# A depthwise convolution as a two-way filter on VectorE, its last tile one step earlier, and output banks evacuated in pairs

## The chip, the cores and the metric

The kernel runs on one core of one Trainium2 chip. The metric is the device time of one execution in microseconds (us); lower is better. Times of the kernel before: 845.77 us, the median of three runs from 844.53 to 849.2. One more execution was profiled, and every row below is from it.

## The reference

One layer of a hybrid decoder, for 1024 positions of a prompt and 8 single new positions of other sequences (1032 rows), with a model width of 1024. All arrays are float32.

```
h = rmsnorm(x) * norm_g
z = h @ w_in                       # 1024 -> 6144: a_val, a_gl, a_gate, b_u, b_v, b_gate
a_in   = a_val * sigmoid(a_gl)
a_conv = causal depthwise conv of a_in, 31 taps per channel, + conv_b
a_out  = silu(layernorm(a_conv)) * silu(a_gate)
gated  = W_s @ layernorm(b_v) + b_s      # per head, inside chunks of 128 positions
b_out  = b_u * gated * silu(b_gate)
y = rmsnorm(x + concat(a_out, b_out) @ w_out) * final_g
```

For the new positions the convolution continues from 30 stored rows, and the chunk has length 1. Outputs are y, the new convolution states and the v rows of the last chunk.

## The kernel before, in words

Channels lie on the 128 partitions, positions along the free dimension. The input projection is computed by a Strassen-like scheme with seven products (`PRODS`) over 2 x 2 blocks. Each float32 factor is split into a rounded head and a remainder (ACT makes the head, VectorE the remainder), and each product is made of three matmuls. `units` lists 24 steps: P (value and gate of the convolution branch, 128 channels), v (256 channels of b_v), B (b_u and b_gate of a head), G (256 channels of a_gate). A step has seven slots, one per product, of 24 matmuls each; in the slots of one step the weights of the next are summed (`wsum`) and split (`wsplit`), and weights of the step after are loaded (`wload`). The first slot of the next step finishes the step before (`finish`).

The order of all instructions on each engine is written out by hand: an engine's queue gets them in the order in which the program text issues them. A planner keeps two counters, `est["pe"]` and `est["dve"]`, to which the text adds hand-set costs, and a queue `fill` of work that can be put anywhere. `pump(margin, pe_ok)` issues items of `fill` while VectorE's counter is less than TensorE's plus the margin; an item of kind "pe" needs `pe_ok`, a "delay" waits until TensorE's counter has advanced, and "bar" waits until the last projection step has been issued (`opened`). Items come out of `fill` in order, so tile k's convolution is issued before tile k+1's.

The convolution is this work. When a P step is finished, `apad` holds 30 zeros and the 1032 positions of a channel tile, and `conv_items(k, apad)` puts the tile's instructions into `fill`. For tiles 0 to 6, ACT computes taps 0 and 1 into two sums (`c`, `accb`), VectorE adds taps 2 to 21 to one or the other by a multiply-add each (L356), ACT computes taps 22 to 30 as products (`prod`, L364), and accumulating DMAs on POOL's queue add these up in two chains (L368) and then onto `c` (L382). For tile 7 (`GTS` is 0) VectorE does taps 2 to 30. `fin` adds the two sums (L379). `acc_item` adds each `c` to a sum over channels by DMA and stores `c` in DRAM.

`ln_items` is put into `fill` after tile 7: mean (a matmul with a matrix of 1/1024, `lnm`), eight centred tiles, their squares and the sum of these (`lnq`), variance (`lnv`), then after "bar" the broadcast of the reciprocal deviation (`lnb`, L466), and for each tile a multiply and silu (`mixa_norm`), a multiply with the gate and the split for the output product (`mixa_gate`, `prep_m`). Tiles that were stored go back and forth by SP's DMAs (`lnload`, `mixa_load`).

The output projection has three groups of columns (384, 384, 264); each has half 1 (the B branch) and then half 0 (the convolution branch), of eight slots `nt` with 24 matmuls each (L677). Half 1 of group 0 needs no LayerNorm, half 0 needs all eight tiles of it. Two slots share a PSUM tile of two banks (`pt[g]`). In half 0 a bank is evacuated in the slot after it (`evac_o`: add to x, L689, square on ACT, L693, sum of squares, L695). Output weights are loaded three slots ahead (`load_w`) and split two slots ahead (`split_w`: `wh` on ACT, L643, `wl` on VectorE, L645).

All large SBUF tiles come from one pool of 51 slots (`U`); an instruction that takes a slot waits until the slot's last user is done.

Of the kernel before, what the change touches and what calls it, by code (L numbers as in the profile page):

```python
# [11 lines left out]
AF = mybir.ActivationFunctionType  # L12
ALU = mybir.AluOpType

D = 1024
NP_ = 1024
NS = 8
NT = NP_ + NS
# [7 lines left out]
CW = 31  # L26
H = CW - 1
EPS = 1e-6
GTS = (9,) * 7 + (0,)
NU = 51  # L30
MMT = 0.12
KEEP_C = (4, 5, 6, 7)
# [10 lines left out]
def body(ctx, tc, xT, w_in, w_out, state, stateT, conv_w, vecs, wsT, w00, b_s,  # L43
# [7 lines left out]
    def U(shape, name, dt=F32):  # L51
        return pool.tile(shape, dt, tag="u", name=name, bufs=NU)
# [4 lines left out]
    def C(shape, name, dt=F32):  # L57
        return cpool.tile(shape, dt, name=name)
# [4 lines left out]
    V = nc.vector  # L63
    A = nc.scalar
    T = nc.tensor
    G = nc.gpsimd
# [10 lines left out]
    cw = C([128, 8, CW], "cw")  # L77
    w00t = C([8, 8], "w00t")
    dW = C([8, 8, 8], "dW")
    csmp = C([128, 8, 8], "csmp")  # L80
    xrs = C([128, 2, 12], "xrs")
    st6 = C([128, 8, 4, 6], "st6")
# [43 lines left out]
    def slot_end():  # L126
        slotno[0] += 1
        while outq and outq[0][0] <= slotno[0]:
            outq.popleft()[1]()


    units = [(n[0], int(n[1])) for n in ("P0 P1 v0 v1 P2 v2 v3 P3 G0 B0 P4 B1 B2 P5 B3 P6 B4 P7 B5 B6 B7 G1 G2 G3"
                                         ).split()]
    mts = {"P": lambda k: (8 + k, k), "v": lambda j: (32 + 2 * j, 33 + 2 * j), "B": lambda h: (40 + h, 24 + h),
           "G": lambda q: (16 + 2 * q, 17 + 2 * q)}
# [183 lines left out]
    cc = {}  # L319
    lnc = {}  # L320

    def acc_item(k):
# [11 lines left out]
            G.dma_start(cD[k], c)  # L334
        fill.append(("dve", 1.15 if k == 7 else 0.0, acc))

    def conv_items(k, ap):
        st = {}
        gt = GTS[k]

        def start():
            c = U([128, NT], f"c{k}")
            cc[k] = c
            st["c"] = c
            st["b"] = U([128, NP_], f"accb{k}")
            A.activation(c[:, :NP_], ap[:, 0:NP_], AF.Identity, scale=cw[:, k, 0:1],  # L346
                         bias=vec[:, CB, k:k + 1])
            A.activation(st["b"], ap[:, 1:1 + NP_], AF.Copy, scale=cw[:, k, 1:2])
            V.scalar_tensor_tensor(out=c[:, NP_:], in0=ap[:, H + NP_:H + NT], scalar=cw[:, k, H:CW],
                                   in1=csmp[:, k, :], op0=ALU.mult, op1=ALU.add)  # L350
        fill.append(("dve", 0.15, start))

        def tap(j):
            def f():
                o = st["c"][:, :NP_] if j % 2 == 0 else st["b"]
                V.scalar_tensor_tensor(out=o, in0=ap[:, j:j + NP_], scalar=cw[:, k, j:j + 1],  # L356
                                       in1=o, op0=ALU.mult, op1=ALU.add)
            return f

        def gtap(j):  # L360

            def f():
                p = U([128, NP_], f"prod{k}_{j}")
                A.activation(p, ap[:, j:j + NP_], AF.Copy, scale=cw[:, k, j:j + 1])  # L364
                if j < CW - gt + 2:
                    st["g", j % 2] = p
                else:
                    G.dma_start(st["g", j % 2], p, accum_op=ALU.add)  # L368
            return f
        for j in range(2, CW - gt):  # L370
            fill.append(("dve", 1.2, tap(j)))
            if gt and j % 2 == 0 and j < 2 + 2 * gt:
                fill.append(("dve", 0.0, gtap(CW - gt + j // 2 - 1)))
            if j == 10 and k:
                acc_item(k - 1)

        def fin():
            c = st["c"]
            V.tensor_tensor(out=c[:, :NP_], in0=c[:, :NP_], in1=st["b"], op=ALU.add)  # L379
            if gt:  # L380
                for e in range(2):
                    G.dma_start(c[:, :NP_], st.pop(("g", e)), accum_op=ALU.add)  # L382
        fill.append(("dve", 1.15, fin))


    ln = {}
# [300 lines left out]
    def evac_o(g, nt):  # L687
        y = yt[g, nt // 2][:, nt % 2, :]
        V.tensor_tensor(out=y, in0=po.pop((g, nt)), in1=y, op=ALU.add)  # L689
        if nt == 0:  # L690
            osq[g] = U([128, 2, GWS[g]], f"osq{g}")
        q = osq[g]
        A.activation(q[:, min(nt, 1), :], y, AF.Square)  # L693
        if 0 < nt < 7 + (g < 2):
            V.tensor_tensor(out=q[:, 0, :], in0=q[:, 0, :], in1=q[:, 1, :], op=ALU.add)  # L695
        dve(0.9)
# [50 lines left out]
    def spatial_b(stt):  # L747
        for q in range(2):
            ks = slice(4 * q, 4 * q + 4)
            V.tensor_tensor(out=stt[q], in0=stt[q], in1=cw[:, ks, None, :H].to_broadcast([128, 4, 8, H]), op=ALU.mult)  # L750
            V.tensor_reduce(out=csmp[:, ks], in_=stt[q], axis=mybir.AxisListType.X, op=ALU.add)
        V.tensor_tensor(out=csmp, in0=csmp, in1=vec[:, CB, :, None].to_broadcast([128, 8, 8]), op=ALU.add)
        V.tensor_tensor(out=dW, in0=ident[:8, None, :8].to_broadcast([8, 8, 8]),
                        in1=w00t[:, :, None].to_broadcast([8, 8, 8]), op=ALU.mult)
        dve(5.0)
# [22 lines left out]
    with tc.manual_schedule():  # L778
# [208 lines left out]
        opened.append(True)  # L987


        pend = None  # L990
        tags = "abce"
        pt = {}
        for s, (g, half, nt) in enumerate(ow):
            if half == 1:
                if nt % 2 == 0:
                    pt[g] = PS(tags[nt // 2], f"po{g}_{nt}")
                po[g, nt] = pt[g][:, nt % 2, :GWS[g]]
            mmo(s, range(0, 2))
            if s:
                wh.pop(s - 1)  # L1000
                wl.pop(s - 1)
            if pend:
                evac_o(*pend)
                pend = None
            load_w(s + 3)
            split_w(s + 2)
            if half == 0 and nt == 0:
                load_xr(g)
            for _ in range(2):
                if oq:  # L1010
                    oq.popleft()()
            if half == 0 and nt == 0:
                for kt in range(8):
                    m_.pop((g, 1, kt))
            if half == 1 and nt == 0 and g:
                for kt in range(8):
                    m_.pop((g - 1, 0, kt))
            mmo(s, range(2, 5))
            if half == 1:
                if g > 0 and nt == 1:  # L1020
                    stat_o(g - 1, "e")
                if g > 0 and nt == 2:
                    bcast_o(g - 1, "e")
                if g > 0 and 3 <= nt < 6:
                    norm_o(g - 1, range(3 * nt - 9, min(3 * nt - 6, 8)))
                if g == 0:
                    pump(1.0 if nt < 5 else 1e9, nt < 6)
                    while outq:
                        slot_end()
                else:  # L1030
                    prep_m(g, 0, nt)
            elif g < 2:
                if nt == 0:
                    for q in range(4):
                        load_m(g + 1, q)
                elif nt > 1 and nt < 6:
                    prep_m(g + 1, 1, 2 * nt - 4)
            if half == 1 and g == 0:
                pump(1.0, nt < 6)
            mmo(s, range(5, 8))  # L1040
            if half == 0:
                pend = (g, nt)
        evac_o(*pend)
        stat_o(2, "a")
        bcast_o(2, "b")
        norm_o(2, range(8))
# [44 lines left out]
```

## Time and profile before

| | before |
|---|---|
| median of three runs | 845.77 us |
| profiled execution | 846.36 us |
| its span, first to last instruction | 844.0 us |
| TensorE busy | 761.8 us (90%) |
| VectorE busy | 652.0 us (77%) |
| ScalarE (ACT) busy | 412.0 us (49%) |
| GpSimd (POOL) busy | 77.4 us (9%) |
| mean granted TensorE clock | 0.944 |

Busy times are of the whole span; matmuls overlap, so a busy TensorE is not TensorE at its peak. The idle time of an engine that is not the bound of a stretch costs nothing. Below, L12 is line 12 of the kernel before; PE is TensorE, DVE is VectorE. A waiting time names the instruction that came last before the waiting one could start.

### The profile page before, as it was taken

The page shows a single profiled execution, that of the slowest core. Times are in us where ns is not written, and L with a number is a line of the kernel's source. Part 1 is how long each engine was busy: PE and PEld are TensorE (multiplying, and loading weights), DVE is VectorE, ACT ScalarE, POOL GpSimd, SP SyncE. Part 2 cuts the span into 40 slices and gives each one's busy share as a digit, 9 for nine tenths or more (in the row PEclk, how much of TensorE's full clock was granted, in tenths as well). Part 3 has the DMA queues.
Part 4 walks back from the last instruction along what each step waited for, and adds up shares of the span by engine and source line. Part 5 has one row for each costly group of instructions (what it writes and reads, how often), then busy time and mean ns, then how long its engine had stood idle before and what let it go on. Part 6 is the DMA issues. An engine that isn't in the chain of part 4 may idle for free.

```text
span 844.0 us, 14083 instructions
## 1 busy us (share of the span) xinstructions
PE 761.8 (90%) x5720; PEld 747.5 (89%) x5720; DVE 652.0 (77%) x786; ACT 412.0 (49%) x561; POOL 77.4 (9%) x96
## 2 busy tenths in 40 slices
PE   6798999989979999999999999999937299999995
PEld 6797999989979999999999999999836289999994
DVE  4747899978977898999899989997575755725843
ACT  3443456555547476565666664334433435214531
POOL 1010001112012112021120211000001000000000
PEclk7768999999989999999999999999968599999998
DMA  8013137767667979678689795436686323663541
GB/s 308 0 64 129 52 102 154 187 162 182 165 188 172 251 167 213 156 195 201 150 178 223 144 244 153 132 126 225 237 338 232 104 89 101 235 220 121 162 189 52
DMA packets 64776, 141.48 MB, mean 168 GB/s; under 512 B 7144, under 2 KB 28328, under 8 KB 64696
## 3 DMA queue, kind: packets, MB, share of 16 engines
q1 hardware_dynamic: 53624, 100.15, 34.4%
q0 software_dynamic: 11088, 40.43, 24.8%
q8 instruction: 45, 0.74, 0.4%
q14 instruction: 19, 0.16, 0.1%
HBM read 80.41 MB, written 24.38 MB: 124 GB/s over the span
## 4 chain that ended last, share of the span: by engine, by line
PE 51%; DVE 11%; DMA 5%; ACT 4%; issue 3%; POOL 0%; SPq 0%; DVEq 0%; ACTq 0%; POOLq 0%
PE po L677 18%; PE zb L269 13%; PE za L269 9%; PE ze L269 4%; PE zc L269 4%; DVE c L356 1%; PE gp L576 1%; DMA c<-prod 1%; DMA wc<-wcD 1%; DMA prod<-prod 1%; DVE accb L356 1%; DVE lnq L431 1%; DVE L L165 1%; DVE yt L689 1%; DVE wl L645 1%
## 5 line engine op out<-in xcount | busy, mean ns | idle before, releaser
L677 PE MATMUL po<-mh,wh 128*128 128x384 f32 (+1 forms) x384 | 125.3, 326 | 25.7 <-ACT wh L643 18.4
L677 PE MATMUL po<-ml,wh 128*128 128x384 f32 (+1 forms) x384 | 123.6, 322 | 0.2 <-DVE ml L668 0.2
L677 PE MATMUL po<-mh,wl 128*128 128x384 f32 (+1 forms) x384 | 123.5, 322 | 0.3 <-DVE wl L645 0.3
L165 DVE TENSOR_TENSOR L<-R,H 128x1024 fp32r<-128x1024 f32 x72 | 87.8, 1221 | 30.1 <-ACT H L164 30.1
L356 DVE SCALAR_TENSOR_TENSOR c<-apad,cw,c 128x1024 f32<-128x1024 f32 x85 | 108.7, 1279 | 1.2 <-ACT c L346 1.2
L356 DVE SCALAR_TENSOR_TENSOR accb<-apad,cw,accb 128x1024 f32<-128x1024 f32 x84 | 107.4, 1278 | 0.0
L677 PEld LDWEIGHTS po<-mh,wh 128*128 128x128 f32 x384 | 72.8, 190 | 29.4 <-ACT wh L643 18.7
L269 PE MATMUL zb<-hT,H 128*128 128x258 f32 x384 | 82.3, 296 | 10.2 <-ACT zb L916 4.5
L164 ACT ACTIVATE H<-R 128x1024 fp32r<-128x1024 f32 x72 | 75.4, 1051 | 26.9 <-DVE R L152 10.7
L364 ACT ACTIVATE prod<-apad,cw 128x1024 f32<-128x1024 f32 x63 | 71.9, 1144 | 22.4 <-DMA prod<-prod 7.2
L269 PE MATMUL zb<-lT,H 128*128 128x258 f32 x384 | 80.0, 291 | 0.5 <-DVE lT L255 0.5
L645 DVE TENSOR_TENSOR wl<-wr,wh 128x1024 fp32r<-128x1024 f32 x48 | 58.6, 1223 | 28.1 <-ACT wh L643 28.0
L269 PE MATMUL zb<-hT,L 128*128 128x258 f32 x384 | 80.0, 290 | 0.0
L269 PE MATMUL za<-lnB,H 128*128 128x258 f32 x384 | 78.3, 285 | 1.0 <-DVE lnB L239 1.0
L269 PE MATMUL za<-hnB,H 128*128 128x258 f32 x384 | 78.5, 286 | 0.0
L269 PE MATMUL za<-hnB,L 128*128 128x258 f32 x384 | 78.1, 285 | 0.0
L677 PEld LDWEIGHTS po<-mh,wl 128*128 128x128 f32 x384 | 72.7, 189 | 0.8 <-DVE wl L645 0.8
L677 PEld LDWEIGHTS po<-ml,wh 128*128 128x128 f32 x384 | 72.8, 190 | 0.5 <-DVE ml L668 0.5
L269 PEld LDWEIGHTS zb<-hT,H 128*128 128x128 f32 x384 | 62.1, 198 | 11.5 <-ACT H L164 4.8
L269 PE MATMUL zb<-hnB,HL 128*128 128x258 f32 x384 | 66.5, 285 | 4.8 <-DVE row L303 2.7
L368 POOL DMA_DIRECT2D prod<-prod x49 | 42.3, 863 | 281.4 <-ACT prod L364 234.1
L269 PEld LDWEIGHTS zb<-lT,H 128*128 128x128 f32 x384 | 62.1, 198 | 0.7 <-DVE lT L255 0.7
(167 smaller groups left out, 1593.4 us busy)
## 6 DMA issues: line engine op xcount, KB each, us to landing
prod<-prod POOLq DMA_DIRECT2D x49, 512.0 KB, 5.7
R<-w_in SPq DMA_DIRECT2D x96, 256.0 KB, 5.4
wr<-w_out SPq DMA_DIRECT2D x48, 512.0 KB, 5.2
c<-prod POOLq DMA_DIRECT2D x14, 512.0 KB, 5.2
x<-xT SPq DMA_DIRECT2D x8, 516.0 KB, 6.4
mbD<-row SPq DMA_DIRECT2D x8, 516.0 KB, 2.6
vD<-va SPq DMA_DIRECT2D x8, 512.0 KB, 4.4
vh<-vD SPq DMA_DIRECT2D x8, 512.0 KB
```

Source lines behind the costliest of these rows:

```text
L164: A.activation(h, r, AF.Copy)
L165: V.tensor_tensor(out=l, in0=r, in1=h, op=ALU.subtract)
L269: T.matmul(z[:, s, :PW], lhsT=HL[u, wi][we][:, wh, cs], rhs=F[name, p][xe][:, kt, :], start=first, stop=(kt == 3 and we == 1), skip_group_ ...
L356: V.scalar_tensor_tensor(out=o, in0=ap[:, j:j + NP_], scalar=cw[:, k, j:j + 1], in1=o, op0=ALU.mult, op1=ALU.add)
L364: A.activation(p, ap[:, j:j + NP_], AF.Copy, scale=cw[:, k, j:j + 1])
L368: G.dma_start(st["g", j % 2], p, accum_op=ALU.add)
L431: V.tensor_tensor(out=ln["q"], in0=ln["q"], in1=ln.pop(("s", k)), op=ALU.add)
L576: T.matmul(p[:, c // 4, 128 * (c % 4):128 * (c % 4) + 128], lhsT=vh[h][:, c, :], rhs=wc[h][:, 0, :], start=True, stop=True)
L645: V.tensor_tensor(out=wl[s], in0=r, in1=wh[s], op=ALU.subtract)
L677: T.matmul(z, lhsT=w[:, cs], rhs=m_[g, half, kt][e], start=(half == 1 and kt == 0 and e == 0 and w is wh[s]), stop=(half == 0 and kt == KT ...
L689: V.tensor_tensor(out=y, in0=po.pop((g, nt)), in1=y, op=ALU.add)
```

## The change

`conv_items` is rewritten. VectorE now computes taps 1 to 20 as ten pairs by a two-way fast filter: even and odd outputs share the product of the sum of a pair's two weights with one sample, and each adds its own product of one weight with a difference of neighbouring samples. So there are three sums of 512 (`m`), each of ten taps, in place of two sums over 1024 with ten taps each: ACT makes the first tap of each, VectorE the nine others, and the two differences `d` come first. The sample operand of the shared sum and both inputs of the differences are read with a step of two, and `fin` writes even and odd outputs with a step of two. The 11 other taps (0 and 21 to 30) are ACT products that DMAs add up, now for all eight tiles; for tile 7 `fin` adds the two DMA sums on VectorE. The weights' pair sums (`cws`) are made once. In `units`, P3 to P7 stand one place earlier. In half 1 of group 0 the planner's margin is 8.0 in place of 1.0. In half 0 of the output projection both banks of a pair are evacuated after the second.

```diff
-GTS = (9,) * 7 + (0,)
+    cws = C([128, 8, 10], "cws")
-    units = [... "P0 P1 v0 v1 P2 v2 v3 P3 G0 B0 P4 B1 B2 P5 B3 P6 B4 P7 B5 B6 B7 G1 G2 G3"
+    units = [... "P0 P1 v0 v1 P2 v2 P3 v3 G0 P4 B0 B1 P5 B2 P6 B3 P7 B4 B5 B6 B7 G1 G2 G3"
+    NF = 10
     def conv_items(k, ap):
+        HN = NP_ // 2
+        others = [0] + list(range(2 * NF + 1, CW))
         def start():
+            d = U([128, 2, HN + NF - 1], f"d{k}")
+            st["d"] = d
+            n = 2 * (HN + NF - 1)
+            for e in range(2):
+                V.tensor_tensor(out=d[:, e, :], in0=ap[:, 1 + 2 * e:1 + 2 * e + n:2], in1=ap[:, 2:2 + n:2],
+                                op=ALU.subtract)
+            mm_ = U([128, 2, HN], f"m01_{k}")
+            st["m"] = [mm_[:, 0, :], mm_[:, 1, :], U([128, HN], f"m2_{k}")]
+            for e in range(3):
+                A.activation(st["m"][e], src(e, 0), AF.Copy, scale=wt(e, 0))
+        fill.append(("dve", 1.25, start))
+        def src(e, i):
+            return ap[:, 2 + 2 * i:2 + 2 * i + NP_:2] if e == 0 else st["d"][:, e - 1, i:i + HN]
+        def wt(e, i):
+            return cws[:, k, i:i + 1] if e == 0 else cw[:, k, 2 * i + e:2 * i + e + 1]
+        def taps(i):
+            def f():
+                for e in range(3):
+                    V.scalar_tensor_tensor(out=st["m"][e], in0=src(e, i), scalar=wt(e, i), in1=st["m"][e],
+                                           op0=ALU.mult, op1=ALU.add)
+            return f
+        def gtap(n):
...
+        n = 0
+        for i in range(1, NF):
+            while n * (NF - 1) < i * len(others):
+                fill.append(("dve", 0.0, gtap(n)))
+                n += 1
+            fill.append(("dve", 2.0, taps(i)))
+            if i == 4 and k:
+                acc_item(k - 1)
+        def fin():
             c = U([128, NT], f"c{k}")
             cc[k] = c
...
+            for e in range(2):
+                V.tensor_tensor(out=c[:, e:NP_:2], in0=m[0], in1=m[1 + e], op=ALU.add)
+            for e in range(2):
+                g = st.pop(("g", e))
+                if k < 7:
+                    G.dma_start(c[:, :NP_], g, accum_op=ALU.add)
                 else:
+                    V.tensor_tensor(out=c[:, :NP_], in0=c[:, :NP_], in1=g, op=ALU.add)
+        fill.append(("dve", 1.4 if k < 7 else 3.7, fin))
...
+        V.tensor_tensor(out=cws, in0=cw[:, :, 1:2 * NF:2], in1=cw[:, :, 2:2 * NF + 1:2], op=ALU.add)
...
-            if pend:
-                evac_o(*pend)
-                pend = None
+            for x in pend:
+                evac_o(*x)
+            pend = []
...
-                    pump(1.0 if nt < 5 else 1e9, nt < 6)
+                    pump(8.0 if nt < 5 else 1e9, nt < 6)
...
-                pump(1.0, nt < 6)
+                pump(8.0, nt < 6)
...
-            if half == 0:
-                pend = (g, nt)
-        evac_o(*pend)
+            if half == 0 and nt % 2:
+                pend = [(g, nt - 1), (g, nt)]
+        for x in pend:
+            evac_o(*x)
```

## Rows read from the trace of the kernel before

**Rows 1.** Busy time by stretch: start:end, length, engines (count), clock, DMA share, GB/s
```profile
100.00:588.50 488.50, 475.42 (x3913) 471.15 (x3912) 442.12 (x513) 275.09 (x379) 65.91 (x79) 0.99 0.70 176
588.50:670.90 82.40, 45.36 (x240) 42.19 (x238) 52.39 (x53) 36.01 (x42) 2.19 (x2) 0.77 0.63 230
670.90:844.00 173.10, 157.04 (x1000) 153.23 (x1000) 93.70 (x135) 59.09 (x86) 3.28 (x4) 0.97 0.43 144
```
**Rows 2.** PE's waits, 588.5 to 670.9: total us, times, longest
```profile
PE po L677 <- ACT wh L643: 18.4, 1, 18.4
PE lnv L443 <- DVE lnq L431: 13.7, 1, 13.7
```
**Rows 3.** The chain that ended last: start us, length us, what
```profile
591.86 1.73 PE lnm L400 x4
...
629.93 3.71 PE lnv L443 x18
...
635.73 3.80 PE lnb L466 x16
641.32 1.25 DVE ma L486
...
670.89 6.71 PE po L677 x28
678.24 8.68 PE po L677 x48
```
**Rows 4.** DVE in time order: convolution of tile 0 starts, tile 7's input, start, end
```profile
109.81 0.21 DVE L349 SCALAR_TENSOR_TENSOR c<-apad,cw,csmp 128x8 f32<-128x8 f32 x1
...
462.33 1.21 DVE L603 TENSOR_TENSOR apad<-apad,row 128x1032 f32<-128x1032 f32 x1
...
515.76 0.22 DVE L349 SCALAR_TENSOR_TENSOR c<-apad,cw,csmp 128x8 f32<-128x8 f32 x1
...
577.54 1.22 DVE L379 TENSOR_TENSOR c<-c,accb 128x1024 f32<-128x1024 f32 x1
```
**Rows 5.** DVE in time order: from start to start at 516, 512 and 1024 elements
```profile
20.02 2.75 DVE L223 SCALAR_TENSOR_TENSOR x<-x,vec,xr 128x516 f32<-128x516 f32 x4
22.68 1.48 DVE L239 SCALAR_TENSOR_TENSOR lnB<-x,hnB 128x516 fp32r<-128x516 f32 x2
...
494.22 0.69 DVE L152 TENSOR_TENSOR R<-R,R 128x512 f32<-128x512 f32 x1
494.82 1.28 DVE L356 SCALAR_TENSOR_TENSOR accb<-apad,cw,accb 128x1024 f32<-128x1024 f32 x1
496.02 1.28 DVE L356 SCALAR_TENSOR_TENSOR c<-apad,cw,c 128x1024 f32<-128x1024 f32 x1
```
**Rows 6.** DMA: packets, MB, share of 16 engines; then issues, KB, us to landing
```profile
q0 software_dynamic: 11088, 40.43, 24.8%
...
prod<-prod POOLq DMA_DIRECT2D x49, 512.0 KB, 5.7
...
c<-prod POOLq DMA_DIRECT2D x14, 512.0 KB, 5.2
```
**Rows 7.** ACT: two passes over 1024 in order, and the group of passes over 512
```profile
410.97 2.18 ACT L364 ACTIVATE prod<-apad,cw 128x1024 f32<-128x1024 f32 x2
...
L164 ACT ACTIVATE HL<-R 128x512 fp32r<-128x512 f32 x24 | 15.0, 625 | 9.9 <-DMA c<-prod 5.2 <-DVE R L152 3.7 <-DMA cD<-c 1.0
```
**Rows 8.** Waits of ACT (100 to 588.5) and of SP's queue (whole span)
```profile
ACT H L164 <- DMA prod<-prod: 9.6, 5, 4.0
...
SPq L145 <- DVE L L165: 77.9, 14, 13.9
```
**Rows 9.** PE's waits, 670.9 to the end: total us, times, longest
```profile
PE po L677 <- DVE yt L689: 7.3, 12, 0.7
```
**Rows 10.** DVE in the last group: evacuation of one bank, its sum of squares
```profile
826.59 0.42 DVE L689 TENSOR_TENSOR yt<-po,yt 128x264 f32<-128x264 f32 x1
...
827.57 0.43 DVE L695 TENSOR_TENSOR osq<-osq 128x264 f32<-128x264 f32 x1 [0.55 <-ACT osq L693]
```

More of the change, by code (lines that the diff above doesn't have):

```diff
@@ L129, in slot_end @@
             outq.popleft()[1]()
-    units = [(n[0], int(n[1])) for n in ("P0 P1 v0 v1 P2 v2 v3 P3 G0 B0 P4 B1 B2 P5 B3 P6 B4 P7 B5 B6 B7 G1 G2 G3"
+    units = [(n[0], int(n[1])) for n in ("P0 P1 v0 v1 P2 v2 P3 v3 G0 P4 B0 B1 P5 B2 P6 B3 P7 B4 B5 B6 B7 G1 G2 G3"
                                          ).split()]
@@ L335, in acc_item, with f @@
         fill.append(("dve", 1.15 if k == 7 else 0.0, acc))
+    NF = 10
     def conv_items(k, ap):
         st = {}
-        gt = GTS[k]
+        HN = NP_ // 2
+        others = [0] + list(range(2 * NF + 1, CW))
         def start():
+            d = U([128, 2, HN + NF - 1], f"d{k}")
[20 more added lines that the diff above has]
+        def gtap(n):
+            def f():
+                j = others[n]
+                p = U([128, NP_], f"prod{k}_{j}")
+                if n == 0:
+                    A.activation(p, ap[:, j:j + NP_], AF.Identity, scale=cw[:, k, j:j + 1], bias=vec[:, CB, k:k + 1])
+                else:
+                    A.activation(p, ap[:, j:j + NP_], AF.Copy, scale=cw[:, k, j:j + 1])
+                if n < 2:
+                    st["g", n] = p
+                else:
+                    G.dma_start(st["g", n % 2], p, accum_op=ALU.add)
+            return f
+        n = 0
[7 more added lines that the diff above has]
+        def fin():
@@ L342, in start @@
             c = U([128, NT], f"c{k}")
             cc[k] = c
[L344 to L348, printed above, removed]
+            m = st.pop("m")
             V.scalar_tensor_tensor(out=c[:, NP_:], in0=ap[:, H + NP_:H + NT], scalar=cw[:, k, H:CW],
                                    in1=csmp[:, k, :], op0=ALU.mult, op1=ALU.add)
-        fill.append(("dve", 0.15, start))
@@ L353, in tap @@
[L353 to L366, printed above, removed]
-                else:
-                    G.dma_start(st["g", j % 2], p, accum_op=ALU.add)
-            return f
@@ L370, in conv_items @@
[L370 to L382, printed above, removed]
@@ L383, in conv_items @@
-        fill.append(("dve", 1.15, fin))
+            for e in range(2):
[4 more added lines that the diff above has]
+                    G.dma_start(c[:, :NP_], g, accum_op=ALU.add)
+                else:
+                    V.tensor_tensor(out=c[:, :NP_], in0=c[:, :NP_], in1=g, op=ALU.add)
+        fill.append(("dve", 1.4 if k < 7 else 3.7, fin))
     ln = {}
@@ L1001, in body @@
                 wl.pop(s - 1)
-            if pend:
-                evac_o(*pend)
-                pend = None
+            for x in pend:
+                evac_o(*x)
+            pend = []
             load_w(s + 3)
```

## The prediction

> **What bounds the kernel now.** I read the busy shares by stretch first, to see where TensorE is not the bound, then TensorE's waits in that stretch, then the chain of waits through it, then VectorE's order of work, to see why the chain is late. Three stretches matter [rows 1]. From 100 to 588.5 us (the input projection) TensorE is busy for 475.4 of 488.5 us, so 13.1 us are idle, and VectorE is busy for 442. From 588.5 to 670.9 (first half of the first output group) it is busy for only 45.4 of 82.4, at a mean granted clock of 0.77, between the two levels (1.2 and 2.4 GHz). From 670.9 to the end it is nearly full again. The middle stretch is where time can be had. Its two long TensorE waits are 18.4 us for `wh`, ACT's rounded copy of an output weight, and 13.7 us for `lnq` [rows 2]. The copy itself is short; it is queued on ACT behind the LayerNorm work. The chain [rows 3] shows that work: mean at 591.9, variance at 629.9, broadcast at 635.7, first multiply of the mixer tiles at 641.3, TensorE in full work again at 670.9. All of it starts after the last convolution tile is done, and that tile is late because of VectorE: its input was ready at 462.3, its convolution began at 515.8, when VectorE was through with the tile before, and ended at 577.5 [rows 4]. So VectorE's convolution backlog sets the start of the LayerNorm, and through it the 82.4 us.
>
> **VectorE's convolution.** Start to start, a multiply-add over 1024 elements takes 1.20 us, an add over 512 takes 0.60, and four multiply-adds over 516 take 2.66, 0.665 each [rows 5]. An add over 1024 is 1.22 long [rows 4]. Before, a tile is 20 multiply-adds (24.0), one add (1.2) and a small one (0.1): 25.3; the last tile has 29 and costs 36.1; together 213. After, a tile is two subtractions of 521 (1.2), 9 x 3 multiply-adds of 512 (18.0), two adds of 512 (1.2) and the small one: 20.5; the last has two adds of 1024 more, 22.9; together 166. That is 47 us less on VectorE. The new instructions read or write every second element, which no row shows. Below, a strided one costs no less than the contiguous 0.665, since it handles as many elements; above, it costs what its whole range would, 1.20. I take 0.665, the row with the same element count. The Trainium skill (Advanced Engine Details and Errata, SBUF Cachelines) says that SBUF works in 16-byte lines and gives full rate if each line is hit at least twice; a step of two fp32 values hits each line twice, so by it the sum stays. No run here shows that yet.
>
> Convolution now runs from 109.8 to 577.5 and gets 213 of these 468 us, 45%. At that share 166 us take 366, up to 476, if the inputs are there. The last tile's input comes one projection step earlier: the first tile's convolution starts at 109.8, as soon as its input is there, 16 steps before 462.3, so a step is 22 us and the input comes at about 440; its 22.9 us then take 50, up to 490. The centring, squares and sums (15 VectorE instructions of 1.2) take another 40 at that share, and with the two TensorE products and the planner's pauses the statistics are done near 545. The code holds the broadcast back until the last projection step is issued (588.5), so some 40 us of slack remain, and a convolution that is up to 40 us later than this still gives the same gain.
>
> **The middle stretch after.** What is left in it: 8 slots of TensorE at 24 matmuls (48 took 8.68 us [rows 3]): 34.7 us; the broadcast; and the eight mixer tiles. With a margin of 8 the planner issues three or four of these tiles at once in the first slot, ahead of the next weight split on VectorE and ACT. So I don't expect TensorE's pace. The broadcast's matmuls come 2.7 us into the stretch (15 of the first slot's 24 matmuls); they took 3.8 at the lowered clock, say 2.5 at the full one, and 1.8 passed from their end to the first multiply [rows 3], which so starts at about 7. From first multiply to TensorE's restart took 29.6 us [rows 3]; the splits of 6 slots, 1.2 each, which then had to wait and now lie between, add 7, and their ACT halves, not wholly hidden, about 2. That makes 45.5 us in place of 82.4: **-36.9**. Ends: 36.9 us if only TensorE's matmuls and broadcast count (-45.5), 54 if the loads of the ten stored tiles come 8 us late (-28).
>
> Mean and variance move into the projection and still cost TensorE their own time, 3.5 with the ACT copy between its two parts, and 3.7 at the lowered clock, say 2.5 at the full one [rows 3]: **+6**. Ends 0 (they fall into idle time) and 20 (a wait as long as the 13.7 of [rows 2] moves with them).
>
> **The projection stretch.** Nine accumulating DMAs a tile over seven tiles (49 + 14) become nine for each of eight and two for seven (72 + 14): 23 more. The software queue moved 40.43 MB in 24.8% of 844 us of all 16 DMA engines [rows 6], so 512 KB cost 2.7 us and 23 cost 62. The DMA share of this stretch goes from 0.70 to 0.83. ACT has 11 passes over 1024 per tile as before, 1.09 each, and three over 512 more, 0.6 each; the last tile has nine long passes more [rows 7]. That is 24 us, beside TensorE's work: ACT is busy for 275 of the 488.5 us [rows 1]. A tile's first multiply-adds wait for the three short passes as the old ones waited for two long ones, and the one sum of weights (80 elements) comes before the first tile: nothing for these. DMA time reaches TensorE by held buffers: ACT's `H` and SP's weight loads wait for slots that `prod` still holds [rows 8], and a tile now holds three slots of the pool (differences and sums) in place of two. Of 209 us of accumulation 13.1 us of idle came out at most, 6%; 6% of 62 is **+4**. Ends: -8 (VectorE's relief takes most of the idle away) and +62 (all of it shows). One step of order (v3 and P3, B and P) only exchanges steps of the same length.
>
> The last tile's two accumulated halves are added on VectorE, in its queue, behind a DMA chain whose links land after 5.7 us [rows 6]. Weight splits are queued behind it, and TensorE waits for those; two slots of lead (a step of 22 us has seven slots, so 6 us) cover most: **+2**, ends 0 and 6. The loads of centred tiles now share SP's queue with weight loads, which wait up to 13.9 us there [rows 8]; VectorE would stand behind them: **+2**, ends 0 and 18 (six loads, 3 each).
>
> **Pairs of banks.** TensorE waits 12 times, 7.3 us in all, for the evacuation of the first bank of a pair while it fills the second [rows 9]. With both evacuated afterwards the next matmuls go to another tile: **-7.3**, at most that and at least none. Next late would be the weight split behind two evacuations, but it has a slot to spare. At the very end the evacuation of bank 6, which ran beside the last slot, moves behind it: add, square, add took 1.4 us (826.59 to 828.0 [rows 10]): **+1.4**.
>
> **Sum.** 846.4 (the profiled execution, span 844.0 and 2.4 around it) - 36.9 + 6 + 4 + 2 + 2 - 7.3 + 1.4 = 817.6. The median of the runs is 0.6 below the profiled one, so **817**.
>
> **Rivals.**
> *TensorE's pace* (797 to 806): half 1 runs at its matmuls' pace (8.6 less) and the projection's idle shrinks (12 less). For it: VectorE's two multiplies for each of eight tiles (19) and its splits (8 of 1.2) are under 36.9. Against: ACT and VectorE alternate on each tile, and the early issue puts splits behind.
> *Accumulations bind* (about 837). At the planner's pace the convolution wants 100 software transfers (the 86 and 14 of the sum and the stored tiles) of 2.7 in 366 us, 270, beside three quarters of the other 133 us of DMA in this stretch: 370 of 366. If the chain of accumulations then holds buffers for a third of its added 62 us, TensorE loses 20. For it: waits of ACT on `prod` exist already. Against: 40 us of slack, and the planner's order lets the last tiles wait for inputs anyway.
> *Strided access is slow* (about 860, the other side). Each strided instruction takes 1.20 instead of 0.665: two subtractions, nine multiply-adds and two adds of a tile cost 7.2 more, 57 over eight tiles. The planner counts 2.0 per three multiply-adds and would fill VectorE past its time; it is in order, the weight splits come late, and TensorE loses what VectorE's free time (46 us in the whole stretch, some 12 of it in the steps with a backlog) doesn't take: 45. 817 + 45 = 862. It decides from 29 us on, 3.6 a tile, when a strided instruction takes half as long again. Against it: the operand has no more elements than the row at 0.665, and a fixed rate per element is what the rows at 512, 516 and 1024 show.
> *The gain isn't there* (about 842): the statistics don't finish before 588.5, since loads and pauses hold them, and the chain stays behind the projection; the bank pairs alone give 6 and a shorter chain little. It needs all 40 us of slack gone.
>
> **Numbers.** Forecast 56% (own range 806 to 829), TensorE's pace 14%, accumulations 15%, strided 7%, gain not there 5%, the rest 3%. Faster by over 0.5%, about what a measurement can tell: below 841.5. The first three and a little of the fourth make 0.87, within 0.5% 0.05, slower 0.08. The range 797 to 841 leaves out the slow side and the best tail.
>
> **What would show it.** Right: multiply-adds of 512 spaced 0.66 to 0.67; the last convolution's adds near 490 and variance near 540; TensorE restarting some 45 us after the projection; no `yt` waits; accumulations at 86 and a DMA share near 0.83 with idle in the projection under 25 us. Wrong: strided rows near 1.2, a VectorE that has no gaps until 588, variance after 588, or TensorE idle of over 35 us in the projection behind `prod` or `lc`.

## The result and the profile after

The changed kernel takes 872.17 us (median of four runs, 870.86 to 873.94), against 845.15 for the kernel before in the same rounds (median of four): a ratio of 1.031 with a 95% interval of 1.027 to 1.036. It is slower by 27 us; 817 was forecast, and the result lies outside the range of 797 to 841. The profiled execution took 872.84 us, its span is 871.1, its mean granted clock 0.941.

I split the span as in [rows 1], at the first matmul of the output projection (588.5 before, 659.3 after) and where TensorE is in full work again (670.9 and 705). Busy time by stretch, after, with the columns of [rows 1]:

```profile
100.00:659.30 559.30, 499.95 (x3923) 490.66 (x3923) 414.32 (x602) 308.33 (x421) 88.22 (x104) 0.95 0.76 188
659.30:705.00 45.70, 39.19 (x214) 37.07 (x212) 34.02 (x35) 25.59 (x31) 0.00 (x0) 0.96 0.72 253
705.00:871.00 166.00, 155.65 (x1001) 154.84 (x1000) 92.81 (x136) 59.82 (x87) 3.28 (x4) 0.96 0.45 152
```

The gains came: the middle stretch went from 82.4 to 45.7 us (-36.7), the rest from 173.1 to 166.0 (-7.1). The projection went from 488.5 to 559.3: +70.8. Of that, 46.3 us are idle time of TensorE (13.1 before, 59.4 now) and 24.5 are busy time, at a granted clock of 0.95 where it was 0.99. VectorE, which the change was to relieve, is busy for 28 us less there (414 for 442), in a stretch that is 71 us longer: it is now waiting.

What TensorE and ACT wait for in the projection (us in total, times, longest) shows where that idle time starts. First after, TensorE:

```profile
PE zb L269 <- DVE apad L303: 15.7, 5, 5.7
PE zb L269 <- ACT zb L944: 14.8, 5, 5.2
PE zb L269 <- DVE row L303: 7.8, 6, 1.9
```

These are waits for the evacuation of a PSUM bank, and they are long now: the largest three of before were 4.5, 2.7 and 2.2 us in all. The evacuating engines are not short of time. ACT, after:

```profile
ACT prod L381 <- DMA prod<-prod: 40.6, 12, 10.2
...
ACT H L164 <- DMA prod<-prod: 11.9, 4, 5.0
ACT prod L381 <- DMA cD<-c: 11.1, 4, 4.6
```

In these three groups ACT waits 64 us to write into pool slots that a running DMA still holds. Before, the same three made 20 us: the 9.6 of `H` in [rows 8], and

```profile
ACT prod L364 <- DMA prod<-prod: 7.2, 4, 3.4
...
ACT prod L364 <- DMA cD<-c: 2.8, 1, 2.8
```

All waits of ACT for a DMA in this stretch went from 40 to 76 us. POOL's queue shows what holds them (32.5 us before, 80.0 after), and the DMA rows the transfers (packets, MB, share of 16 engines; then issues, KB, us to landing):

```profile
POOL prod L385 <- DMA prod<-prod: 80.0, 23, 8.3
```
```profile
q0 software_dynamic: 14400, 52.49, 30.9%
...
prod<-prod POOLq DMA_DIRECT2D x72, 512.0 KB, 6.2
...
c<-prod POOLq DMA_DIRECT2D x14, 512.0 KB, 4.6
```

86 accumulations were issued, as counted, and they land after 6.2 us where it was 5.7 [rows 6]. One stall in order of time (start, length, what; in brackets the idle time before and its releaser):

```profile
424.94 0.86 POOL L385 DMA_DIRECT2D prod<-prod  x1 [8.33 <-DMA prod<-prod]
...
428.94 1.14 ACT L381 ACTIVATE prod<-apad,cw 128x1024 f32<-128x1024 f32 x1
...
433.13 1.06 ACT L164 ACTIVATE H<-R 128x1024 fp32r<-128x1024 f32 x1 [3.04 <-issue]
433.70 0.83 POOL L385 DMA_DIRECT2D prod<-prod  x1 [5.09 <-DMA prod<-prod]
434.22 1.22 DVE L165 TENSOR_TENSOR L<-R,H 128x1024 fp32r<-128x1024 f32 x1 [4.81 <-ACT H L164]
435.36 0.69 DVE L303 TENSOR_TENSOR apad<-zb,p 128x516 f32<-128x516 f32 x1
...
436.10 0.80 PE L269 MATMUL zb<-hnB,HL 128*128 128x258 f32 x2 [5.69 <-DVE apad L303]
```

Read it from the end. TensorE stood for 5.69 us until VectorE emptied a bank (435.36); VectorE is in order and stood for 4.81 behind a weight's remainder `L`; that waited for ACT's weight head `H`, which began at 433.13, just as the accumulation issued at 424.94 landed (the next one of the same chain, which waits for it, goes at 433.70; the one at 427.74, left out here, is the tile's other chain's). The rows give no releaser for this `H`, but the trace of the run holds the semaphores: ACT's queue waits 5.84 us, from 427.25 to 433.09, for those of a weight load, which had last moved at 420.74, and of the accumulation issued at 424.94, whose last part landed at 433.06. So this `H` waited for a slot that a transfer held for 8.1 us. An in-order ACT carries the wait from a full pool to weights, VectorE and TensorE. That the other long waits come about in the same way is a reading from the sums: VectorE's waits for `H`, before and after, doubled too.

```profile
DVE L L165 <- ACT H L164: 26.9, 20, 4.0
DVE L L165 <- ACT H L164: 56.8, 28, 5.2
```

After the stall the clock is down as well. The granted clock (column behind POOL's) was at its upper level (2.4 GHz) in the 10 us before the stall and at the lower one (1.2 GHz) just behind it:

```profile
420.00:430.00 10.00, 10.00 (x85) 10.00 (x85) 8.43 (x13) 7.26 (x9) 1.72 (x2) 1.00 1.09 277
436.00:439.00 3.00, 2.90 (x13) 2.90 (x14) 3.00 (x6) 1.72 (x5) 0.85 (x1) 0.50 1.06 220
```

So the busy time of the projection grows with its stalls.

The rest of the forecast shows up. The chain through the LayerNorm, after (start, length, what), which answers [rows 3]:

```profile
559.72 2.00 PE lnm L427 x4
...
611.36 1.80 PE lnv L470 x18
...
662.58 1.80 PE lnb L493 x16
...
666.16 1.25 DVE ma L513
```

Mean and variance are inside the projection, 46 us before its end, though 70 us later than I wrote. And no TensorE wait for `yt` [rows 9] is left from the projection's end on; the largest are:

```profile
PE po L704 <- ACT wh L670: 3.9, 2, 2.0
PE po L704 <- DVE wl L672: 1.9, 3, 0.6
```

### The profile page after: what moved, and what is told of

Same layout as the page of the kernel before. It is cut to its first block, busy times and chain, and to the rows that moved or that the text cites. A ratio compares the mean times of both kernels' runs of the same rounds, so it can differ in the third digit from the quotient of the medians.

```text
span 871.1 us, 14256 instructions
## 1 busy us (share of the span) xinstructions
PE 777.8 (89%) x5720; PEld 762.3 (88%) x5720; DVE 606.4 (70%) x860; ACT 435.9 (50%) x594; POOL 97.5 (11%) x119
## 3 DMA queue, kind: packets, MB, share of 16 engines
q0 software_dynamic: 14400, 52.49, 30.9%
## 5 line engine op out<-in xcount | busy, mean ns | idle before, releaser
L381 ACT ACTIVATE prod<-apad,cw 128x1024 f32<-128x1024 f32 x80 | 90.7, 1146 | 64.7 <-DMA prod<-prod 40.6
L269 PE MATMUL zb<-hT,H 128*128 128x258 f32 x384 | 84.8, 304 | 25.2 <-ACT zb L944 14.8
L369 DVE SCALAR_TENSOR_TENSOR m<-d,cw,m 128x512 f32<-128x512 f32 x144 | 101.5, 747 | 0.0
L385 POOL DMA_DIRECT2D prod<-prod x72 | 62.4, 866 | 308.5 <-ACT prod L381 198.8
L269 PE MATMUL zb<-hnB,HL 128*128 128x258 f32 x384 | 73.6, 308 | 23.6 <-DVE apad L303 15.7
L269 PEld LDWEIGHTS zb<-hT,H 128*128 128x128 f32 x384 | 64.2, 205 | 27.8 <-ACT zb L944 15.8
L269 PEld LDWEIGHTS zb<-hnB,HL 128*128 128x128 f32 x384 | 60.4, 210 | 26.4 <-DVE apad L303 16.9
L269 PE MATMUL zb<-lT,H 128*128 128x258 f32 x384 | 82.2, 298 | 0.7 <-DVE lT L255 0.7
L269 PE MATMUL zb<-hT,L 128*128 128x258 f32 x384 | 82.3, 297 | 0.0
L269 PEld LDWEIGHTS zb<-lT,H 128*128 128x128 f32 x384 | 64.4, 205 | 1.0 <-DVE lT L255 1.0
```

The costliest lines, as they stand in the source:

```text
L269: T.matmul(z[:, s, :PW], lhsT=HL[u, wi][we][:, wh, cs], rhs=F[name, p][xe][:, kt, :], start=first, stop=(kt == 3 and we == 1), skip_group_ ...
L369: V.scalar_tensor_tensor(out=st["m"][e], in0=src(e, i), scalar=wt(e, i), in1=st["m"][e], op0=ALU.mult, op1=ALU.add)
L385: G.dma_start(st["g", n % 2], p, accum_op=ALU.add)
```

## The experiments

The theory after this reading: the accumulating DMAs bind, through the pool slots that they hold. Rivals: the order of the steps, the planner's pace (a tile's convolution is issued too early), the chain in itself (each accumulation waits for the one before it, so a tile's eleven cost their landing times one after the other), or VectorE's strided work. All ratios are to the kernel before in the same rounds, with 95% intervals. The projection runs from 100 us to the first output matmul: 488.5 us before, 559.3 after.

**Accumulations left out (`e4_noacc`)**, the others in place. The sum over the DMA-added taps is left out.

```diff
-                else:
-                    G.dma_start(st["g", n % 2], p, accum_op=ALU.add)
```


> The changed kernel without the accumulating DMAs of products 2 to 10 of each tile (72 of 86; the products are still made on ACT, their sum is left out). Accumulations (the chains of DMAs and the products that hold pool slots while they wait): TensorE's idle in the projection falls from 59 us to about 15, the projection ends near 600 instead of 661, in all about 810. Rival, the order of steps or the extra pool slots of the filter: the products' slots are free sooner, but the order and the three slots per tile are the same, so the projection still ends after 640 and the time stays above 850.

817.34 us, 0.966 (0.962 to 0.971); projection 505.6. All 72 products are still made by ACT. So order, pace, strided work and ACT's load are not the cause of most of the loss; the transfers, or what they hold, are.

**The same transfers without accumulation (`e6_dram`)**: each product goes to a DRAM buffer of its own (its sum is left out).

```diff
-                    G.dma_start(st["g", n % 2], p, accum_op=ALU.add)
+                    G.dma_start(scr[k][n], p)
```


> The changed kernel with the 72 accumulating DMAs replaced by 72 plain DMAs of the same 512 KB on the same queue, each to a DRAM buffer of its own (the sum of products is left out). So the bytes and the issues stay, and no transfer waits for the one before it. If the serial chain is what binds: idle falls as without them, time 810 to 825. If the DMA engines' time as such binds: a DMA share still near 0.8 in the projection, idle of 40 us or more, time above 850.

813.52 us, 0.962 (0.957 to 0.966). Its stretches (columns as above) and its DMA rows:

```profile
100.00:600.20 500.20, 480.82 (x3924) 473.31 (x3924) 413.22 (x602) 308.01 (x421) 65.64 (x104) 0.99 0.64 210
600.20:645.00 44.80, 37.70 (x212) 35.28 (x210) 33.42 (x34) 24.75 (x30) 0.00 (x0) 1.00 0.74 253
645.00:810.50 165.50, 155.09 (x1002) 153.86 (x1002) 93.35 (x136) 60.61 (x88) 3.28 (x4) 0.97 0.45 153
```
```profile
q0 software_dynamic: 14400, 52.49, 20.2%
...
scr<-prod POOLq DMA_DIRECT2D x72, 512.0 KB, 4.6
```

The same bytes and the same number of transfers cost almost nothing: bytes are not the cause. Against the changed kernel the projection is 59 us shorter, 40 of them idle time (59.4 to 19.4) and 19 TensorE's busy time for the same matmuls, at 0.99 for 0.95. So a third of the loss is not waiting but slower matmuls after the waits, as in the stall above. ACT's three waits for slots, 64 us in the changed kernel, are 20 here. With 28 others the 72 transfers took 269 us of 16 engines when they accumulated (30.9% of 871.1) and 164 here (20.2% of 810.6): 1.5 us less for each. The edit changes two things at once, the accumulation and the target (DRAM in place of SBUF).

**Plain transfers in a chain (`e12_dramchain`)**: two DRAM buffers a tile in turn, so that each waits for the last but one.

```diff
+                    G.dma_start(scr[k][n % 2], p)
```


> As the run with plain DMAs to DRAM, but a tile's nine transfers go to two DRAM buffers in turn, so that each waits for the one before it on the same buffer (the sum of products is left out). Chain without accumulation. If products hold slots because each transfer waits for the one before: time 835 to 870, idle in the projection over 30 us. If it is the accumulating transfer's own engine time (2.7 us for 512 KB against some 1.4 for the plain one): as without the chain, 813 within 8.

818.61 us, 0.970 (0.964 to 0.976); projection 505.5, landing after 4.3 us. The chain is there, since POOL waits for it:

```profile
POOL scr L386 <- DMA scr<-prod: 49.2, 18, 6.1
```

Its order by itself costs 5 us against `e6_dram`, so as a cause of its own that rival falls. Each link is shorter here than an accumulating one (6.2 us), so a chain of links as long as those was not run.

**Four chains (`e7_4chains`)**: products added onto four sums a tile instead of two, which two more accumulations then join.

```diff
-                if n < 2:
+                if n < 4:
...
-                    G.dma_start(st["g", n % 2], p, accum_op=ALU.add)
+                    G.dma_start(st["g", n % 4], p, accum_op=ALU.add)
...
+            for e in range(2):
+                G.dma_start(st["g", e], st.pop(("g", e + 2)), accum_op=ALU.add)
```


> The changed kernel with four chains of products per tile in place of two: 11 accumulating DMAs a tile as before (seven onto four products, two that join chains in pairs, two onto c), so the number, kind and bytes of transfers stay, while a chain has two links instead of four or five; two more pool slots are held by first products. If the serial wait of one accumulation for the one before on the same product is the cause: idle in the projection falls from 59 us to under 35, time 825 to 845. If the engine time of accumulating transfers is: the same idle, 865 to 875. If pool slots are what is short in themselves: more idle, over 875.

932.89 us, 1.103 (1.096 to 1.110); projection 621. Two more slots a tile and shorter chains made it much worse, with the same number of accumulations. That points at slots as what is short.

**Fewer slots**: the pool cut from 51 to 49, in the changed kernel (`e9_nu49`) and in the kernel before (`e13_before49`).

```diff
-NU = 51
+NU = 49
```


> The changed kernel with 49 pool slots instead of 51. If products that wait in the chain reach TensorE through the slots they hold: two slots fewer cost as much as two products more that wait, some 10 to 25 us more, 882 to 897. If slots play no part and ACT or VectorE wait for the DMAs by the data alone: 872 within 4.

> The kernel before with 49 pool slots instead of 51. If its 51 slots are just enough: the projection grows by 30 to 60 us and the time to 870 to 900. If it has slots to spare, so that the change alone made them short: 845 to 855.

After: 940.46 us, 1.111 (1.105 to 1.117), +68, 34 us a slot, far more than the 10 to 25 that I expected for both. Before: 882.73 us, 1.046 (1.039 to 1.052), +39, 19 us a slot. The kernel before was already on the slope; the changed one stands where it is steeper. The projections of `e13_before49` and, below it, of `e9_nu49`:

```profile
100.00:624.80 524.80, 490.97 (x3931) 484.40 (x3931) 444.05 (x514) 276.81 (x380) 65.74 (x79) 0.97 0.66 165
```
```profile
100.00:728.00 628.00, 526.02 (x3990) 514.36 (x3989) 422.78 (x613) 312.59 (x425) 88.07 (x104) 0.92 0.68 169
```

With fewer slots and the same DMAs, TensorE has more idle time (33.8 in place of 13.1; 102 in place of 59.4), a lower granted clock, and the DMA engines a smaller share (0.66 for 0.70, 0.68 for 0.76): they are not what is full.

**The kernel before with one slot more a tile (`e14_slot`)**, held from the first tap to the end and never used for anything, and **with more accumulations (`e8_before11`)**, 63 + 14 in place of 49 + 14, whose 11 products a tile are also spaced anew; both have the old convolution.

```diff
+            st["x"] = U([128, NP_], f"more{k}")
+            V.memset(st["x"][:, :8], 0.0)
...
+            V.memset(st.pop("x")[:, :8], 0.0)
```


> The kernel before with one more pool slot held by each tile's convolution from its start to its end (a slot that is touched with two small memsets and does nothing); DMAs, order, taps as before. If the filter's third slot is a good part of the loss: 865 to 885. If only the products' chains count: under 852.

```diff
-GTS = (9,) * 7 + (0,)
+GTS = (11,) * 7 + (0,)
...
-            if gt and j % 2 == 0 and j < 2 + 2 * gt:
-                fill.append(("dve", 0.0, gtap(CW - gt + j // 2 - 1)))
+            while n * (CW - gt - 2) < (j - 1) * gt:
+                fill.append(("dve", 0.0, gtap(CW - gt + n)))
+                n += 1
```


> The kernel before with 11 instead of 9 of 31 taps as products by DMA for tiles 0 to 6 (18 instead of 20 on VectorE), nothing else changed: 63 accumulations become 77. If the accumulations alone are the cause: idle in the projection grows from 13 us to 30 or more, while VectorE's 17 us less bring the LayerNorm forward; in all 845 to 865. If the filter's form, the order or the margin are: idle stays at 13 and the time falls to about 835.

The idle slot: 860.16 us, 1.020 (1.014 to 1.025), +16, between my two figures (865 to 885, or under 852); its projection is 507.2, 19 longer than before. The 14 accumulations: 853.26 us, 1.009 (1.006 to 1.011), but its projection is 516.3, 28 longer than before, of which VectorE's relief gives a part back in the middle stretch. That is 2.0 us for each accumulation with its product, against 0.06 times 2.7 in my sum. Scaled to 23 it is 46; with 19 for the slot and 6 for the moved mean and variance that makes 71, as much as was measured. This sum is an estimate, not a proof, and that it meets the figure is in part chance: the new order of steps, 8 us of the projection (`e5_order`, below), is not in it, and with plain transfers the same extra slot cost little (`e6_dram`), so the two costs are not independent.

**Fewer products.** With 12 pairs on VectorE a tile has 7 DMA-added taps, with 11 it has 9, with 13 it has 5. `e2_nf12` keeps the new order, the others have the old order of steps.

```diff
-    NF = 10
+    NF = 12
...
-    cws = C([128, 8, 10], "cws")
+    cws = C([128, 8, 12], "cws")
```


> The changed kernel with 12 pairs (24 taps) on VectorE instead of 10 and 7 products per tile by DMA instead of 11: five chained accumulations a tile instead of nine, 54 in all with the two onto c (63 before the change, 86 after). VectorE does six multiply-adds of 512 more a tile, 4 us, 32 in all. Accumulations as the cause: idle in the projection as before the change or less, statistics done before the projection ends, about 810. Order of steps or pool slots: it stays near 870; VectorE as the bound: about 850.

> The filter with 12 pairs and 7 products by DMA, with the steps in the old order; margin and bank pairs as changed. The old order took 9 us off with 10 pairs. If that was steps with a P between them that give slots time to come free: 813 to 818. If it was particular to the long chains: 820 to 826, as with the new order.

> The filter with 11 pairs and 9 products per tile by DMA (as many as before the change for tiles 0 to 6), steps in the old order, the rest as changed. Between 7 products (811) and 11 (863). If products and their slots set the loss step by step: halfway, 830 to 845, with the projection ending near 620. If the filter's own slot makes most of it: over 850. If it starts only past 9 products: under 820.

> The filter with 13 pairs and 5 products per tile by DMA, old order. From 11 to 9 to 7 products the time fell by 30 and 22. If slots still bind: 795 to 803. If the projection is at TensorE's pace by then and VectorE, with 2 us more a tile, ends the statistics after the projection: 810 to 825.

```diff
-    units = [... "P0 P1 v0 v1 P2 v2 P3 v3 G0 P4 B0 B1 P5 B2 P6 B3 P7 B4 B5 B6 B7 G1 G2 G3"
+    units = [... "P0 P1 v0 v1 P2 v2 v3 P3 G0 B0 P4 B1 B2 P5 B3 P6 B4 P7 B5 B6 B7 G1 G2 G3"
```


> The changed kernel with the steps in the old order (v3 before P3, B0 before P4, and so on), all else as changed. Accumulations as the cause: idle in the projection within 10 us of 59, the statistics some 20 us later, still before the projection ends, time 865 to 878. Order as the cause: idle back near 15, time about 820.

| run | pairs, products | order | time, us | ratio (95%) | projection |
|---|---|---|---|---|---|
| changed | 10, 11 | new | 872.2 | 1.031 (1.027 to 1.036) | 559.3 |
| `e5_order` | 10, 11 | old | 863.4 | 1.020 (1.016 to 1.024) | 551.4 |
| `e18_nf11_old` | 11, 9 | old | 832.8 | 0.987 (0.984 to 0.990) | 518.9 |
| `e10_nf12_old` | 12, 7 | old | 811.4 | 0.961 (0.956 to 0.966) | 501.7 |
| `e17_nf13_old` | 13, 5 | old | 833.5 | 0.987 (0.985 to 0.989) | 502.7 |
| `e2_nf12` | 12, 7 | new | 822.8 | 0.971 (0.966 to 0.976) | 512.4 |

Each step of two products a tile moves the time by 21 to 31 us, until at 13 pairs the other limit is met: VectorE is too late for the statistics (variance at 628, after the projection), and TensorE again waits for `wh`, 20.3 us; neither of my figures for 13 pairs (795 to 803, 810 to 825) was met. At 12 pairs the projection and the middle stretch are both short:

```profile
100.00:601.70 501.70, 484.24 (x3938) 478.37 (x3937) 445.03 (x652) 275.20 (x391) 59.84 (x72) 0.98 0.67 177
601.70:646.00 44.30, 38.71 (x211) 36.92 (x210) 33.02 (x34) 24.25 (x30) 0.00 (x0) 0.96 0.71 246
```

VectorE is as busy as before the change (445 for 442), and that is right: the two-way filter pays as fewer DMA products, not as free VectorE time. The new order costs 9 us with 10 pairs and 11 with 12; why was not taken apart. My figure for 12 pairs in the old order, 813 to 818, was 2 us too high.

**Pace (`e3_pace`)**: the planner counts 2.5 per three multiply-adds.

```diff
-            fill.append(("dve", 2.0, taps(i)))
+            fill.append(("dve", 2.5, taps(i)))
```


> The changed kernel with the planner's cost of three multiply-adds at 2.5 instead of 2.0, so that a tile is spread over about the time that it took before (25.2 of planned VectorE time instead of 20.7); no instruction is added or taken. If the pace of accumulations per time is the cause: idle in the projection falls to 20 to 30 us, the statistics end near 600, time about 830. If the number of transfers alone counts, or the order of steps: within 10 us of 872.

863.52 us, 1.021 (1.016 to 1.026). The projection shrank to 539.4, but variance came after its end (646.8). The 830 that I expected of the pace missed: the time lies within 10 us of 872, the figure that I gave for the number of transfers or the order of steps. Yet the pace counts in the projection, which is 20 us shorter: ACT's `prod` waits 12.9 us there for accumulations in place of 40.6. Most of that is given back in the middle stretch.

**One slot less (`e15_cd`, `e16_best`)**: `c` written into the slot of the differences, in the changed kernel and in the 12-pair one.

```diff
-            c = U([128, NT], f"c{k}")
+            c = st.pop("d").rearrange("p a b -> p (a b)")[:, :NT]
```


> The changed kernel with a tile's result written into the slot of its differences, which are dead by then, so that no fourth slot is taken at a tile's end. DMAs, order and instructions as changed. Slots as what is short: 5 to 20 us less, 852 to 867. If the end of a tile is not where they are short: 872 within 4.

> The filter with 12 pairs, 7 products by DMA, the old order of steps, and the result in the slot of the differences. If slots still cost something at 811: 803 to 810, idle in the projection down from 17 us. If the projection is bound by TensorE there: 811 within 3.

870.67 us, 1.031 (1.027 to 1.035), and 810.87 us, 0.961 (0.958 to 0.963). No clear effect; the 5 to 20 us that I expected in the first missed. So slots are not short at a tile's end: in the program text `c` is taken just as `d` comes free. The second is the best version found, 4% faster than before and 7% faster than the change, and `e10_nf12_old` is as good.

**The two other edits.** Pairs of banks alone, in the kernel before (`e1_pairs`), and the margin of 8 put back to 1 in `e10_nf12_old` (`e19_margin1`).

```diff
-            if half == 0:
-                pend = (g, nt)
+            if half == 0 and nt % 2:
+                pend = [(g, nt - 1), (g, nt)]
```


> The kernel before with only the evacuation of output banks in pairs. The 12 waits of TensorE, 7.3 us, go and the tail gains 1.4: 6 us less, 838 to 840. If another wait takes their place: 844 within 2.

```diff
-                    pump(8.0 if nt < 5 else 1e9, nt < 6)
+                    pump(1.0 if nt < 5 else 1e9, nt < 6)
...
-                pump(8.0, nt < 6)
+                pump(1.0, nt < 6)
```


> The version with 12 pairs and the old order, with the planner's margin in half 1 of group 0 back at 1.0. If the early issue puts weight splits behind mixer tiles: the stretch from the projection's end to half 0 gets shorter, 40 us instead of 45, time 806. If with the small margin the mixer tiles come too late and the rest is issued in one go in the sixth slot: 815 to 825.

836.36 us, 0.991 (0.988 to 0.994): the pairs give 7.5. With the margin at 1, 816.08 us, 0.966 (0.965 to 0.968): the middle stretch is 50.0 in place of 44.3, and the wait for `wh` is back with 10.9. The margin gives 5.

## Why the prediction was wrong

The step that failed is "The projection stretch": **+4** for 23 more accumulating DMAs. It came out at about 65 (70.8 less the 6 of the moved mean and variance), some 8 of it the new order of steps, which the prediction put at nothing. I had named +62 as an end and chosen 6% of it, the share of idle time to accumulation time in the kernel before. That takes an average as the price of the next unit. The runs show what the next unit costs: 2.0 us for each further accumulation with its product (`e8_before11`), and 19 us for each slot less in the kernel before, 34 in the changed one, so a slot is worth more in the fuller pool. `e13_before49` was the measurement that the step needed.

Two more things in that step were wrong. "A tile now holds three slots of the pool in place of two" stood there without a price; `e14_slot` gives 16 us for such a slot. And 62 counted DMA time and idle time only: 19 us more, by the comparison with `e6_dram`, came as busy time at a lower granted clock. The 209 us were not all accumulation either: they are the whole software queue's, and 8 of its 77 transfers are plain copies (`c` to DRAM, and the first one into the sum over channels).

- The middle stretch: 45.7 for a forecast 45.5, and 44.8, 44.3 in `e6_dram` and `e10_nf12_old`. Right. It also holds that the gain needs only the statistics to be done before the projection ends. That they were, with 46 us to spare, was luck in the changed kernel: they came 70 us late, and the projection's end came 71 us late as well.
- VectorE's convolution: duration and rate as taken. In the changed kernel (count, then busy time and mean ns of one):

```profile
L369 DVE SCALAR_TENSOR_TENSOR m<-d,cw,m 128x512 f32<-128x512 f32 x144 | 101.5, 747 | 0.0
L369 DVE SCALAR_TENSOR_TENSOR m<-apad,cws,m 128x512 f32<-128x512 f32 x72 | 53.7, 747 | 0.0
```

  The second reads every second sample and takes the same 747 ns, and start to start both are at 0.66 to 0.67. The rival of slow strided access falls. The Trainium skill (Advanced Engine Details and Errata, SBUF Cachelines) says that two hits on a 16-byte line are enough for the full rate. The trace agrees with it, by these 747 ns.
- The step time: P0 and P7 lie 17 places apart in `units`, not 16, so a step is 20.7 us in place of 22. It moves the last tile's input by 1 us and changes nothing else.
- Mean and variance inside the projection, +6: TensorE's busy time is 480.8 in `e6_dram` for 475.4 before, both at 0.99, so +5.4, with all else that differs there. About right; the variance alone took 1.80 us, less than the 2.5 that I took for it.
- Pairs and tail, -7.3 and +1.4: 7.1 less in the last stretch here, 7.5 alone. Right, a little more than the 5.9. The last add, square and add took 1.4 us, as said.
- The last tile, on VectorE, after (input, then its adds):

```profile
492.31 1.24 DVE L630 TENSOR_TENSOR apad<-apad,row 128x1032 f32<-128x1032 f32 x1 [0.21 <-ACT row L299]
...
545.36 0.69 DVE L403 TENSOR_TENSOR c<-m 128x512 f32<-128x512 f32 x1
545.96 0.69 DVE L403 TENSOR_TENSOR c<-m,m 128x512 f32<-128x512 f32 x1
546.68 2.49 DVE L409 TENSOR_TENSOR c<-c,prod 128x1024 f32<-128x1024 f32 x2
```

  From input to adds it took 53 us, near the 50 of the forecast. The input came 52 us later than the 440 that I wrote, behind the stalls of the projection.
- The two terms of 2 us (the sums of tile 7 behind the DMA chain, the loads on SP) can't be told apart in a projection that lost 71. For the loads `e6_dram` speaks: they are as in the changed kernel there, and it takes 813.5, below my sum. For the sums of tile 7 the row at 546.68 speaks: VectorE has no idle time before them, so nothing of these 2 us shows.

The rival *accumulations bind* had the mechanism and the place and a price of 20 for what cost 65, since it too took a third of the DMA time and no slot. Its "against", 40 us of slack, was no argument: that slack covers a late LayerNorm, and TensorE itself was what stalled. The sign that I had named, idle time of over 35 us in the projection behind `prod`, is what the profile showed, with 59 us.

What stays open: why accumulation hurts where a plain transfer doesn't. It lands later (6.2 us for 4.3 to 4.6) and takes 1.5 us more of 16 engines, and the runs changed both at once, and the target with them. A plain transfer within SBUF was not run, nor the changed kernel with more slots. How the 65 us divide between the extra slot, the extra accumulations and the order of steps isn't settled either.

## What to carry to other kernels

Where buffers come from one full pool, price an offloaded piece of work by the slot it holds times how long, until its transfer has landed, and not by its bytes or its share of DMA time; and measure the slope first, by taking two slots away from the kernel as it is. When VectorE is made cheaper in such a kernel, spend the freed time on taking work back from the DMA queues (here 12 pairs and 7 products: 811 us) before leaving it idle. A stall of TensorE costs more than its idle time when the granted clock falls after it (19 us beside 40 here).

## What the runs showed of the hardware

The software queue's 100 transfers of 512 to 516 KB, 72 of them accumulations of products within SBUF, took 269 us of 16 engines in the changed kernel (30.9% of 871.1) and as much in `e9_nu49` (28.7% of 939.9: 270) and `e7_4chains` (28.8% of 931.7: 268). With those 72 plain and to DRAM they took 164 (`e6_dram`) and 163 (`e12_dramchain`, 20.0% of 816.8), about 1.5 us less for each. The time from issue to landing is less steady: its median for the 72 was 6.2 us in the changed kernel, 5.4 in `e9_nu49` and 6.6 in `e7_4chains`, and 4.6 and 4.3 for the plain ones. A plain chain and plain independent transfers differed by 5 us of the whole time.

A VectorE multiply-add of 512 float32 elements took 747 ns with one operand read with a step of two and without. Behind a stall of TensorE of 5.69 us its granted clock was at the lower level (0.50 of full speed, 436 to 439 us), where it had been at the upper one before the stall.
